# Where the raw blocks of branch a land, when the stored sums are made, and which halvings stand between drains

## The chip, the core and the metric

The kernel runs on one core of one Trainium2 chip. A core has five engines with a queue of instructions each: PE (matrix products and transposes), DVE (vector operations), ACT (activations and copies), POOL (here masks, and the issue of DMAs) and SP (here only the issue of DMAs). Each queue is worked off in order: an instruction that waits holds up everything behind it on its engine. Moved bytes go through 16 DMA engines that all queues share. The metric is the time of the whole kernel on the device in microseconds (us), the median of several runs; less is better.

## What is computed

One layer of a hybrid block over 1024 tokens of width 1024, in float32 arithmetic: a norm, a wide projection, a gated mixer of a short convolution (branch a) and a forgetting attention (branch b), an output projection, and a feed-forward net.

```python
def mixer(h, w_in, b_f, conv_w, w_branch, w_out):
    proj = jnp.einsum("bsd,dn->bsn", h, w_in)
    q, k, v, f_logit, g_b, g_c, hc, gate_conv, gate_attn = jnp.split(proj, _SPLITS, axis=-1)
    ya = g_b * causal_depthwise_conv(g_c * hc, conv_w)
    logf = jax.nn.log_sigmoid(f_logit.astype(jnp.float32) + b_f.astype(jnp.float32))
    yb = forgetting_attention(q.reshape(shp), k.reshape(shp), v.reshape(shp), logf)
    ya_d = jnp.einsum("bsc,cd->bsd", ya, w_branch[0])
    yb_d = jnp.einsum("bsc,cd->bsd", yb, w_branch[1])
    merged = jax.nn.sigmoid(gate_conv) * ya_d + jax.nn.sigmoid(gate_attn) * yb_d
    return jnp.einsum("bsd,de->bse", merged, w_out)

for l in range(DEPTH):
    m = mixer(rmsnorm(x, norm_mix_pre[l]), ...)
    x = x + rmsnorm(m, norm_mix_post[l])
    x = x + rmsnorm(swiglu(rmsnorm(x, norm_ffn_pre[l]), w_gate_up[l], w_down[l]), norm_ffn_post[l])
```

The logits of query i and key j get the bias c[i] - c[j], where c is the running sum of logf. The kernel keeps those rows of c, one per head, spread over all partitions: the forget rows, tiles `cb`.

## The kernel before, in words

**Numbers in two halves.** A float32 operand is kept as a high half (rounded by a copy, mostly on ACT) and a low half (the difference, on DVE); a product is three matmuls, high by high, high by low, low by high (`mm3`). Making both halves is called halving here (`split`, `halve`); what comes from memory is first a raw block and then halved. All engine calls go through one helper, so nearly every row of the profile has the line L76; the names of the tiles (out<-in) say which step it is.

**The stages in time.** Norm and small projections take the first 61 us. Then come 18 jobs up to about 418 us, the large projections by Strassen's scheme: seven products of 512-wide blocks in place of eight. A job has 84 matmuls of 128x512 and takes about 19 us. Its weights arrive as raw blocks (`raw<-in_w_in`, 512 KB each, on SP's queue into a few raw tiles), and DVE and ACT make their sums and halves one job ahead. The last job (`last_pair`) has the first two attention steps in it. From 416 to 566 us runs the attention loop, steps t = 2 to 22: for head pair j and some of its query rows the logits (`sp`), the row maxima on DVE (`row_max`, records CUSTOM_DVE or ISA), the exponentials on ACT (`expo`), the transposes (`tps`, drained into `ptT` by ACT and DVE) and the weighted sum with v (`po`). Each step also has one chunk of branch a (`pba`): the product of w_branch[0] with ya, again by Strassen's scheme, its seven products P1 to P7 for four pieces of the columns. After 566 us come the rest of branch a, branch b, the output projection and the feed-forward net.

**Side work in the jobs.** The sums of blocks that Strassen's scheme needs of w_branch (`wa_steps`), w_out (`wo_steps`) and ya (`ya_steps`) are made during the jobs and stored to memory (`wa_dram`, `wt_dram`, `ya_ops`) for later. Each is a generator in a few pieces. The table `plans` says which piece runs in which job: an entry (job, n) puts the next piece behind the job's addition of c12 (n = 0) or of c21 (n = 1). The raw rows of w_out go into two tiles, r0 and l0, and each piece of them ends with a store that reads them; the next `wo_steps` loads the same two tiles and so waits for those stores. In the jobs a scheduler sets the order of each queue; in the attention loop the program's order is kept on every engine.

**Around the start of attention.** Branch a's first two products need the quarter B11 of ya (P1) and B21 (P2). `load_y` fetches a quarter as a raw block (two DMAs `raw<-ya_dram`) into one of the raw tiles, and `split_y` halves it into `yB` (ACT copies, DVE subtracts). The raw tiles at that time also hold the first two attention steps' probabilities and their transposes, so a load waits for PE to be done with them. `cb_of(j, e)` loads a forget row of the head pair j into one of two `cb` tiles; `load_kv(1)` loads both forget rows, k and v of pair 1.

Of the kernel before, what the change touches and what calls it, by code (L numbers as in the profile page):

```python
# [10 lines left out]
F32 = mybir.dt.float32  # L11
# [6 lines left out]
P = 128  # L18
S = 1024
# [27 lines left out]
def block_kernel(  # L47
# [156 lines left out]
    def h_pair(name, shape):  # L204
        return [h_pool.tile(shape, F32R, name=f"{name}{t}") for t in "hl"]

# [341 lines left out]
    def flat(t):  # L548
        return t.rearrange("p a b -> p (a b)")
# [7 lines left out]
    def raw_t():  # L557
        return wtile("raw", 3)
# [156 lines left out]
    def wo_steps(k):  # L715

        both = []
        for tag, row in (("r0", k), ("l0", k + 4)):
            t = w0_tile(tag, F32)
            nc.sync.dma_start(flat(t), wout_d[row * P : (row + 1) * P, :])  # L720
            both.append(flat(t).rearrange("p (a b) -> p a b", a=2))
# [27 lines left out]
    def half_tile(t):  # L749
        return flat(t).rearrange("p (a b) -> p a b", a=2)  # L750
# [20 lines left out]
    def wa_steps(k):  # L771
# [16 lines left out]
        yield  # L788
        spill(wa_dram, 2, k, u, half_tile(w0_tile("l0")))
        yield  # L790
# [386 lines left out]
    for first, make in (  # L1177
        (((2, 0), (2, 1), (3, 0)), lambda: wa_steps(0)),
        (((3, 1), (4, 0), (4, 1)), lambda: wa_steps(1)),
        (((4, 1), (5, 0), (5, 1), (7, 0)), lambda: wo_steps(0)),  # L1180
        (((7, 1), (8, 0), (8, 1), (10, 0)), lambda: wo_steps(1)),
        (((10, 1), (11, 0), (11, 1), (12, 0)), lambda: wo_steps(2)),
        (((12, 1), (13, 0), (13, 1), (14, 0)), lambda: wo_steps(3)),
        (((10, 1), (11, 1), (12, 0), (12, 1)), lambda: ya_steps(0)),
        (((13, 1), (14, 0), (14, 1), (15, 0)), lambda: ya_steps(1)),
    ):
        it = make()
        for j, n in first:
            plans[j][n].append(it)
# [134 lines left out]
    HOME = dict(B11="h0", B21="h1", T2="l0", T3="l1", T4="h0", T1="h1", B22="l1")  # L1324
    wring, raws = deque(), {}

    def load_y(o, queue=nc.sync):
# [3 lines left out]
        if o in SUMS_Y:  # L1331
            queue.dma_start(f32(t), ya_ops[SUMS_Y.index(o)])
            return
        raws[o] = half_tile(raw_t())
        m, ns = dict(B11=(0, n1), B21=(2, n1), B22=(2, n2))[o]
# [162 lines left out]
    for t, what, p in (  # L1498
# [64 lines left out]
    cuts[2].append(do(split_y, "B21"))  # L1563
    cuts[21].append(do(split_y, "B22"))
    for t, list_ in list(chunks.items()):
        for c in list_:
            o = SEQ[c[0]][0]
            if t > 2 and o not in SUMS_W:
                cuts[t - 1].append(do(split_w, o, c[1]))
    for k, t in enumerate((16, 17, 21, 22)):  # L1570
# [10 lines left out]
    for t in (6, 8, 10, 13, 14, 20, 21, 22):  # L1581
        at[t].append(next_sg)
    at[17].append(late_sgs)
    at[15] += [do(cb_of, 3, 0, True), do(cb_of, 3, 1, True)]
    for k, t in enumerate((13, 13, 16, 16)):
# [9 lines left out]
    next_w()  # L1595
    load_kv(1)
    q_load(1)
    load_y("B21")
    lows = [split_y("B11"), split_w("A11", 0)]
    for low in lows:  # L1600
        low()
    for _ in range(3):
        next_w()
    for _ in range(4):
        next_sg()
    mask_of(2, 0)
    for t in range(2, NU + 2):
# [6 lines left out]
        if t == NU:  # L1614
            for m in [a_chunk(*c) for c in chunks.pop(t)]:
                m()
        if 5 < t <= NU:
# [7 lines left out]
        if t <= 5:  # L1625
            po_copy = pv_pair(t - 2)
        for i, e in now[0]:
            row_max(t, i, e)
        if t < NU and len(steps[t][1]) > 1 and not joined(steps[t][1]):
            mask_of(t, steps[t][1][1])  # L1630
# [888 lines left out]
```

## Time and profile before

| | |
|---|---|
| median of 3 runs | 1334.93 us (1333.1 to 1335.35) |
| the profiled execution | 1335.76 us, of which 1334.0 us lie between its first and last instruction (the span) |
| mean granted PE clock | 0.993 |
| busy share of PE, DVE, ACT, POOL | 98%, 71%, 42%, 15% |
| moved by DMA | 235.64 MB, 177 GB/s in the mean |

All times in this text are from the profiled execution, counted from its first instruction. In a timeline row the columns are start, length, engine, line, operation with out<-in and shapes, how many, and in brackets the idle time just before it with what ended it. SPq and POOLq stand for DMA issues on those queues. "x38" in a table of windows is the number of instructions that began in the window, and PEclk the clock that PE was granted, as a share of the full one.

### The profile page before, as it was taken

Reading aid. Unit: us, or ns where it says so; the run is one execution under the profiler, and the core shown is the slowest. Engines: PE = TensorE matmul, PEld = TensorE weight load, DVE = VectorE, ACT = ScalarE, POOL = GpSimd, SP = SyncE. Lnnn points to the kernel's source line nnn. Section 1 sums busy time; section 2 is a strip of 40 time slices with the busy share of each in tenths; the row PEclk is TensorE's granted clock in tenths of the full one; section 3 lists DMA queues with packets and bytes.
Section 4 is the critical chain, followed back from the end, with each engine's and each line's share of the span. In section 5 each row is a group of like instructions: output and inputs, shape, how many; then the busy total and the mean of one; then the engine's idle time right before and its main releaser. Section 6 shows DMA issues by size and latency. Waiting matters only on the chain.

```text
span 1334.0 us, 17816 instructions
## 1 busy us (share of the span) xinstructions
PE 1307.5 (98%) x6671; PEld 1086.3 (81%) x6671; DVE 948.4 (71%) x1357; ACT 565.1 (42%) x880; POOL 203.0 (15%) x371
## 2 busy tenths in 40 slices
PE   9999999998997999999999999999999999999998
PEld 8988878887886788788888878888888888888886
DVE  7876788785754577887767788867666756677574
ACT  7533232343443677522678433223222323444451
POOL 3111110122212222100223121211011101000001
PEclk9999999999999899999999999999999999999999
DMA  6356544466725564585467556533233327966541
GB/s 230 96 157 205 167 146 155 158 215 238 255 112 181 206 210 161 186 305 205 129 190 234 189 173 203 186 125 102 80 118 103 116 90 257 363 234 194 159 166 63
DMA packets 179638, 235.64 MB, mean 177 GB/s; under 512 B 12232, under 2 KB 121872, under 8 KB 179040
## 3 DMA queue, kind: packets, MB, share of 16 engines
q1 hardware_dynamic: 154544, 150.31, 35.9%
q0 software_dynamic: 24992, 84.20, 17.1%
q8 instruction: 52, 0.85, 0.3%
q14 instruction: 34, 0.28, 0.1%
q10 hardware_dynamic: 16, 0.00, 0.0%
HBM read 164.94 MB, written 69.53 MB: 176 GB/s over the span
## 4 chain that ended last, share of the span: by engine, by line
PE 92%; DVE 4%; DMA 2%; issue 1%; SPq 1%; ACT 0%; DVEq 0%; POOLq 0%; POOL 0%; ACTq 0%
PE b L76 57%; PE pd L76 16%; PE pv L76 3%; PE pbb L76 3%; PE pba L76 3%; PE tps L76 2%; PE po L76 2%; PE sp L76 2%; PE tp L76 1%; DMA raw<-in_w_in_dram 1%; PE ma L76 1%; DVE lo L76 1%; PE mb L76 1%; DMA raw<-ya_dram 1%; SPq L76 1%
## 5 line engine op out<-in xcount | busy, mean ns | idle before, releaser
L76 DVE TENSOR_TENSOR c<-c,b 128x512 f32<-128x512 f32 x215 | 146.8, 683 | 74.0 <-PE b L76 72.8
L76 DVE TENSOR_TENSOR lo<-raw,hi 128x1024 fp32r<-128x1024 f32 (+1 forms) x91 | 109.6, 1205 | 70.1 <-PE b L76 54.3
L76 ACT ACTIVATE hi<-raw 128x1024 fp32r<-128x1024 f32 (+1 forms) x98 | 99.6, 1017 | 100.4 <-PE b L76 53.8
L76 ACT ACTIVATE hi<-sx 128x1024 fp32r<-128x1024 f32 x44 | 46.7, 1062 | 192.8 <-PE b L76 166.7
L76 DVE TENSOR_TENSOR sx<-raw 128x512 f32<-128x512 f32 x78 | 53.7, 688 | 42.8 <-DMA raw<-in_w_in_dram 29.0
L76 DVE TENSOR_TENSOR lo<-sx,hi 128x1024 fp32r<-128x1024 f32 x44 | 53.8, 1223 | 38.6 <-PE b L76 37.4
L76 PE MATMUL b<-w12h,lo 128*128 128x512 f32 x208 | 80.9, 389 | 0.0
L76 PE MATMUL b<-w12h,hi 128*128 128x512 f32 x204 | 79.4, 389 | 0.0
L76 PE MATMUL b<-w12l,hi 128*128 128x512 f32 x204 | 79.4, 389 | 0.0
L76 PE MATMUL b<-hh,hi 128*128 128x512 f32 x176 | 69.0, 392 | 0.7 <-DVE c L76 0.7
L76 PE MATMUL b<-hh,lo 128*128 128x512 f32 x176 | 68.5, 389 | 0.0
L76 PE MATMUL b<-hl,hi 128*128 128x512 f32 x176 | 68.5, 389 | 0.0
L76 PE MATMUL b<-w,s4h 128*128 128x512 f32 x208 | 64.0, 389 | 0.0
L76 PE MATMUL pd<-hi,lo 128*128 128x512 f32 x160 | 62.3, 389 | 0.0
L76 PE MATMUL pd<-hi 128*128 128x512 f32 x160 | 61.9, 390 | 0.0
L76 POOL DMA_DIRECT2D a_dramA<-um x33 | 17.9, 541 | 277.2 <-DVE um L76 276.6
L76 PE MATMUL pd<-ghi 128*128 128x512 f32 x148 | 57.6, 390 | 0.0
L76 PE MATMUL pd<-ghi,glo 128*128 128x512 f32 x148 | 57.6, 389 | 0.0
L76 PE MATMUL pd<-glo,ghi 128*128 128x512 f32 x148 | 57.6, 389 | 0.0
L76 PE MATMUL b<-hT12h,lo 128*128 128x512 f32 x136 | 53.9, 396 | 3.8 <-DVE lo L76 3.7
L76 PE MATMUL b<-hT34h,hi 128*128 128x512 f32 x136 | 53.0, 390 | 0.9 <-DVE c L76 0.9
L76 PE MATMUL b<-hT12h,hi 128*128 128x512 f32 x136 | 53.4, 393 | 0.0
(487 smaller groups left out, 3601.6 us busy)
## 6 DMA issues: line engine op xcount, KB each, us to landing
raw<-in_w_gate_up_dram SPq DMA_DIRECT2D x52, 512.0 KB, 4.1
raw<-in_w_in_dram SPq DMA_DIRECT2D x35, 512.0 KB, 4.8
a_dramS<-um POOLq DMA_DIRECT2D x44, 256.0 KB, 2.9
a_dramA<-um POOLq DMA_DIRECT2D x33, 256.0 KB, 2.6
sg<-sg_dram SPq DMA_DIRECT2D x32, 256.0 KB, 5.6
graw<-a_dramS SPq DMA_DIRECT2D x14, 512.0 KB, 3.7
sg_dram<-c POOLq DMA_DIRECT2D x24, 256.0 KB, 2.5
raw<-in_w_down_dram SPq DMA_DIRECT2D x11, 512.0 KB, 6.1
```

The source lines that it names most:

```text
L76: ins = getattr(self.engine, name)(*args, **kw)
```

## The change

It has six parts, and every operation of before is still there, as often as before.

1. The tiles of `h_pair` get tags of their own, and the pool of the attention tiles sets aside its five `wraw`, two `v` and two `cb` tiles at the start.
2. The eight loads of w_out in the jobs are issued on POOL's queue in place of SP's, and `plans` is written anew: the pieces of one sum are spread over more half-jobs, and fewer sums share a half-job. One piece of the second `wa_steps` uses the tile h0 in place of l0.
3. `load_y` puts B11 and B21 into `cb` tiles (named `yraw`) and only B22 into a raw tile. The two forget rows of pair 1 are loaded in step 3, behind the last read of the raw blocks, and the other loads at the start of attention change places.
4. The low halves of B11 and of its weight, two operations on DVE, stand behind the first row maxima of step 2 in place of ahead of them.
5. In step 17 the copy `rT` stands ahead of the row maxima.
6. At step 21 P6 stands ahead of P5's last piece, B22 is halved between their two drains, and the weight halving of that step is done one step earlier.

```diff
     def h_pair(name, shape):
-        return [h_pool.tile(shape, F32R, name=f"{name}{t}") for t in "hl"]
+        return [h_pool.tile(shape, F32R, tag=f"{name}{t}", name=f"{name}{t}") for t in "hl"]
...
             t = w0_tile(tag, F32)
-            nc.sync.dma_start(flat(t), wout_d[row * P : (row + 1) * P, :])
+            nc.gpsimd.dma_start(flat(t), wout_d[row * P : (row + 1) * P, :])
...
-        spill(wa_dram, 2, k, u, half_tile(w0_tile("l0")))
+        spill(wa_dram, 2, k, u, half_tile(w0_tile(("l0", "h0")[k])))
...
         (((2, 0), (2, 1), (3, 0)), lambda: wa_steps(0)),
-        (((3, 1), (4, 0), (4, 1)), lambda: wa_steps(1)),
-        (((4, 1), (5, 0), (5, 1), (7, 0)), lambda: wo_steps(0)),
-        (((7, 1), (8, 0), (8, 1), (10, 0)), lambda: wo_steps(1)),
-        (((10, 1), (11, 0), (11, 1), (12, 0)), lambda: wo_steps(2)),
-        (((12, 1), (13, 0), (13, 1), (14, 0)), lambda: wo_steps(3)),
-        (((10, 1), (11, 1), (12, 0), (12, 1)), lambda: ya_steps(0)),
-        (((13, 1), (14, 0), (14, 1), (15, 0)), lambda: ya_steps(1)),
+        (((3, 1), (3, 1), (5, 0)), lambda: wa_steps(1)),
+        (((4, 0), (4, 1), (5, 1), (6, 1)), lambda: wo_steps(0)),
+        (((7, 0), (7, 1), (8, 0), (8, 1)), lambda: wo_steps(1)),
+        (((10, 0), (10, 1), (11, 0), (11, 1)), lambda: wo_steps(2)),
+        (((11, 0), (12, 0), (12, 1), (13, 0)), lambda: ya_steps(0)),
+        (((14, 0), (14, 0), (14, 1), (15, 1)), lambda: ya_steps(1)),
+        (((13, 1), (15, 0), (16, 0), (16, 1)), lambda: wo_steps(3)),
...
+    for tag, shape, n in (("wraw", [P, 2, P], 5), ("v", [P, ST, P], 2), ("cb", [P, S], 2)):
+        for _ in range(n):
+            t1.tile(shape, F32, tag=tag, name=tag, bufs=n)
...
-        raws[o] = half_tile(raw_t())
+        raws[o] = half_tile(
+            raw_t() if o == "B22" else t1.tile([P, ST, P], F32, tag="cb", name="yraw", bufs=2)
+        )
...
-        (18, "P4", 3), (19, "P5", 1), (20, "P5", 2), (21, "P5", 3), (21, "P6", 0),
+        (18, "P4", 3), (19, "P5", 1), (20, "P5", 2), (21, "P6", 0), (21, "P5", 3),
...
-    cuts[21].append(do(split_y, "B22"))
...
-                cuts[t - 1].append(do(split_w, o, c[1]))
+                cuts[t - 1 - (t == 21)].append(do(split_w, o, c[1]))
...
+    at[3] += [do(cb_of, 1, 0), do(cb_of, 1, 1)]
...
     next_w()
-    load_kv(1)
-    q_load(1)
     load_y("B21")
-    lows = [split_y("B11"), split_w("A11", 0)]
-    for low in lows:
-        low()
+    first_lows = [split_y("B11"), split_w("A11", 0)]
+    k_load(1)
     for _ in range(3):
         next_w()
-    for _ in range(4):
+    next_sg()
+    load_v(1)
+    q_load(1)
+    for _ in range(3):
         next_sg()
...
-            for m in [a_chunk(*c) for c in chunks.pop(t)]:
-                m()
+            p6, p5 = [a_chunk(*c) for c in chunks.pop(t)]
+            p6()
+            split_y("B22")()
+            p5()
...
+        if turned and t == 17:
+            turned()
+            turned = None
         for i, e in now[0]:
             row_max(t, i, e)
+        if t == 2:
+            for low in first_lows:
+                low()
```

The table, the placing of tiles and the written order move instructions at three places on which much rests.

**SP's queue in jobs 8 to 16, before.** `raw` are the weights of the jobs, `r` and `l` the rows of w_out for the tiles r0 and l0, `rows` two forget rows.

```order
L76 DMA l_2118<-in_w_out_dram 128x1024
L76 DMA raw<-in_w_in_dram 128x8x128 x4
L76 DMA r_2537<-in_w_out_dram 128x1024
L76 DMA raw<-in_w_in_dram 128x8x128 x2
L76 DMA l_2539<-in_w_out_dram 128x1024
L76 DMA raw<-in_w_in_dram 128x8x128 x4
L76 DMA r_2831<-in_w_out_dram 128x1024
L76 DMA l_2833<-in_w_out_dram 128x1024
L76 DMA raw<-in_w_in_dram 128x8x128 x4
L76 DMA rows_970<-c_dram 128x1024 x2
```

SP now holds 24 loads of `raw` in a row there, and the loads of w_out stand on POOL's queue, of which this is the part around jobs 10 to 13:

```order
L76 DMA wt_dram_132<-r_2472 128x1024
L76 DMA sg_dram_136<-so 128x512
L76 DMA wt_dram_133<-h_2688 128x1024
L76 DMA r_2969<-in_w_out_dram 128x1024
L76 DMA sg_dram_136<-c_2635 128x512
L76 DMA sg_dram_136<-c_2614 128x512
L76 DMA sg_dram_136<-c_2598 128x512
L76 DMA wt_dram_133<-l_2474 128x1024
L76 DMA rows_970<-ya_dram_71 128x1024
L76 DMA ya_ops<-yh 128x2x512
L76 DMA rows_970<-ya_dram_73 128x1024
```

A load of r0 or l0 now stands behind the stores of the side work and ahead of stores of the jobs' results (`sg_dram<-c`).

**SP's queue at the start of attention, before.** `qk_dram` holds q and k, `ya_dram_70` and `71` the block B11, `72` and `73` the block B21.

```order
L76 DMA v_3459<-v_dram 128x8x128
L76 DMA raw<-ya_dram_70 128x512
L76 DMA raw<-ya_dram_71 128x512
L76 DMA wraw<-in_w_branch_dram 128x2x128
L76 DMA cb<-c_dram 128x1024 x2
L76 DMA lo<-qk_dram_67 128x1024
L76 DMA v<-v_dram 128x8x128
L76 DMA raw<-qk_dram_67 128x1024
L76 DMA raw<-ya_dram_72 128x512
L76 DMA raw<-ya_dram_73 128x512
L76 DMA wraw<-in_w_branch_dram 128x2x128 x3
```

The same place now:

```order
L76 DMA v_3459<-v_dram 128x8x128
L76 DMA yraw<-ya_dram_70 128x512
L76 DMA yraw<-ya_dram_71 128x512
L76 DMA wraw<-in_w_branch_dram 128x2x128
L76 DMA yraw<-ya_dram_72 128x512
L76 DMA yraw<-ya_dram_73 128x512
L76 DMA lo<-qk_dram_67 128x1024
L76 DMA wraw<-in_w_branch_dram 128x2x128 x3
L76 DMA sg<-sg_dram_135 128x512
L76 DMA v<-v_dram 128x8x128
L76 DMA raw<-qk_dram_67 128x1024
```

The second block of ya went from behind q and v to right behind the first, and the two loads of `cb` stand further down, behind four `sg` and two `wraw`.

**DVE's queue at step 21, before.** `um` are the drains of branch a's chunks, `s4l` a weight halving, `yB` the low half of B22.

```order
L76 TENSOR_TENSOR um<-um,pba 128x512
L76 TENSOR_TENSOR um<-sg,um 128x512
L76 COPY ptT<-tps 128x512
L76 TENSOR_TENSOR s4l<-wraw,s4l 128x256
L76 TENSOR_TENSOR um<-um,pba 128x512 x2
L76 TENSOR_TENSOR um<-sg,um 128x512
L76 COPY ptT<-tps 128x128
L76 RECIPROCAL ri<-rsum 128x8
L76 COPY ptT<-tps 128x512
L76 TENSOR_TENSOR yB_5254<-raw,yB_5254 128x1024
```

The same place now:

```order
L76 TENSOR_TENSOR um<-um,pba 128x512
L76 TENSOR_TENSOR um<-sg,um 128x512
L76 COPY ptT<-tps 128x512
L76 TENSOR_TENSOR um<-um,pba 128x512
L76 TENSOR_TENSOR um<-sg,um 128x512
L76 TENSOR_TENSOR yB_5265<-raw,yB_5265 128x1024
L76 TENSOR_TENSOR um<-um,pba 128x512
L76 COPY ptT<-tps 128x128
```

The weight halving left this stretch for the step before, and the low half of B22 moved up between the two drains, ahead of the transposes' copies.

## The prediction

> **What bounds the kernel now.** I read the page's shares first, then the waits of PE.
>
> ```profile
> span 1334.0 us, 17816 instructions
> PE 1307.5 (98%) x6671; PEld 1086.3 (81%) x6671; DVE 948.4 (71%) x1357; ACT 565.1 (42%) x880; POOL 203.0 (15%) x371
> ...
> PE tps L76 <- ACT ptT L76: 4.9, 1, 4.9
> PE pba L76 <- ACT s L76: 4.6, 1, 4.6
> PE b L76 <- DVE lo L76: 3.7, 1, 3.7
> PE b L76 <- DVE c L76: 1.7, 2, 0.9
> ...
> PE pba L76 <- ACT yB L76: 0.9, 1, 0.9
> PE pba L76 <- DVE s4l L76: 0.9, 1, 0.9
> PE pba L76 <- DVE yB L76: 0.8, 1, 0.8
> PE pba L76 <- DVE rT L76: 0.7, 1, 0.7
> ```
>
> PE is busy for 98% of the span, and the change takes no matmul away, so only two things can shorten the time: PE's few idle stretches, and slow matmuls after them. A row of the second view gives us in total, times, longest. Three single waits are long: one in the jobs (b, for a low half) and two at the start of attention (pba and tps). The rest are below 1 us each. So I followed those three back, each on the queue of its releaser.
>
> **The wait in the jobs.** These are rows of the timelines of POOL, SP, DVE and PE, then two of the chain of waits, one of the DMA issues (its last number is the median us to landing), and one of the table of windows (length, busy us of PE, PEld, DVE, ACT, POOL, granted clock, share of the DMA engines, GB/s).
>
> ```profile
> 298.93 0.57 POOL L76 DMA_DIRECT2D wt_dram<-l  x1 [1.20 <-DVE l L76]
> ...
> 306.33 0.34 SPq L76 DMA_DIRECT2D l<-in_w_out_dram  x1
> 306.78 13.40 SPq L76 DMA_DIRECT2D raw<-in_w_in_dram  x2
> ...
> 302.08 1.23 DVE L76 TENSOR_TENSOR lo<-raw,hi 128x1024 fp32r<-128x1024 f32 x1 [1.83 <-PE b L76]
> ...
> 315.71 0.39 PE L76 MATMUL b<-hT12l,hi 128*128 128x512 f32 x1
> 319.83 0.80 PE L76 MATMUL b<-hT12h,lo 128*128 128x512 f32 x1 [3.73 <-DVE lo L76]
> ...
> 322.98 0.40 PE L76 MATMUL b<-hT12h,hi 128*128 128x512 f32 x1
> ...
> 299.78 5.00 PE b L76 x22
> ...
> 306.78 9.60 DMA raw<-in_w_in_dram
> ...
> raw<-in_w_in_dram SPq DMA_DIRECT2D x35, 512.0 KB, 4.8
> ...
> 300.00:310.00 10.00, 10.00 (x46) 8.29 (x45) 3.99 (x5) 3.87 (x5) 4.18 (x7) 1.00 0.98 333
> ```
>
> Read from the end. PE waits 3.73 us for a low half, the last of a row of DVE operations that began when its raw block had landed (306.78 + 9.60 = 316.38). That raw block could have been fetched when DVE had read its tile (302.08 + 1.23 = 303.3), but SP's queue stood at the load of l0, which waits until the store of the old l0, issued at 298.93, is done. So the block was issued 306.78 - 303.3 = 3.5 us late, among transfers that kept the DMA engines 98% busy. The cost is more than the wait: 22 matmuls usually take 5.00 us, 0.227 each, but from 315.71 to 322.98 only eight begin, 7.27 - 8 x 0.227 = 5.45 us lost. The first seven after the wait ran slow.
>
> By the Trainium skill ("TensorE: Matmul & The Clock Gate", section "What's actually happening") PE falls to half clock after about 3.4 us without work and needs about as long under load to come back, so each such stall would cost up to 1.7 us beyond itself. The trace agrees here: 5.45 - 3.89 (the gap from 315.71 to 319.83 less one matmul) = 1.56.
>
> **The start of attention.**
>
> ```profile
> 398.97 0.37 SPq L76 DMA_DIRECT2D v<-v_dram  x1
> ...
> 418.99 0.81 SPq L76 DMA_DIRECT2D raw<-ya_dram  x2
> ...
> 422.42 3.86 SPq L76 DMA_DIRECT2D raw<-qk_dram  x1
> 426.45 0.79 SPq L76 DMA_DIRECT2D raw<-ya_dram  x2
> ...
> 426.82 7.45 DMA raw<-ya_dram
> ...
> 400.00:410.00 10.00, 10.00 (x50) 7.69 (x48) 5.02 (x8) 2.39 (x4) 1.98 (x4) 1.00 0.25 84
> ...
> 416.35 0.33 PE L76 MATMUL sp<-hi 64*128 64x128 f32 x2
> ...
> 425.38 2.93 PE L76 MATMUL pba<-yB,s 128*128 128x512 f32 x6 [4.58 <-ACT s L76]
> ...
> 436.25 0.90 PE L76 MATMUL tps<-ident,rows 128*128 128x128 f32 x3 [4.86 <-ACT ptT L76]
> ...
> 443.60 0.50 PE L76 MATMUL sp<-hi 64*128 64x512 f32 x2
> ...
> 462.88 0.33 PE L76 MATMUL sp<-hi 64*128 64x128 f32 x2
> ...
> 475.68 0.50 PE L76 MATMUL sp<-hi 64*128 64x512 f32 x2
> ```
>
> SP issues nothing between 399 and 419, since B11 goes into a raw tile that PE still reads, while the DMA engines are a quarter busy. Then ten loads go out at once. B11 is issued at 418.99, and PE's first branch chunk waits 4.58 us for it. B21 is issued at 426.45, behind a q load that held the queue for 3.86 us, and takes 7.45 us to land; ACT, in order, halves it ahead of the copy `ptT`, for which PE waits 4.86 us. Steps 2 and 3 are rows (5, 0) and (4, 1) of pair 0; steps 7 and 8 are the same rows of pair 1, with chunks of the same six matmuls. From the first logits of step 2 to those of step 4 it is 443.60 - 416.35 = 27.25 us, from step 7 to step 9 it is 475.68 - 462.88 = 12.80. So 14.45 us are lost: 4.58 + 4.86 = 9.44 of idling and 5.0 of slow matmuls (six in 2.93 us).
>
> By the same rule of the skill the two stalls would lose at most 9.44 + 2 x 1.7 = 12.8 us. The rows say 14.45, and I take the rows; by the rule the forecast below would be 1.6 us later.
>
> **What each part does to the time.** *Loads of w_out on POOL, new plans.* SP's queue holds only weights there, so the raw block goes out at 303.3; even with the same 9.60 us it lands at 312.9, and the 3.5 us saved nearly cover the 3.73 us lost. The new table has the second ya sum and the last w_out sum elsewhere, so the fetch has fewer neighbours. Bounds: nothing, if the DMA engines are as full in another way, and 5.45. I take 5.4, because a block 0.2 us late leaves no clock to lose. Of the two waits for `c`, the 0.9 us one in job 6 comes from a copy of l0 that waited for its load; l0 is now fetched two pieces ahead. Bounds 0 and 0.9, I take 0.7. The other 0.8 us in that row lies behind the attention and stays. The price of eight more issues on POOL is read from the nearest row:
>
> ```profile
> L76 POOL DMA_DIRECT2D sg_dram<-c x24 | 13.1, 545 | 67.7 <-ACT c L76 64.5 <-DVE c L76 3.2
> ```
>
> 8 x 0.545 = 4.4 us on an engine that is 15% busy: nothing, as long as no load stands waiting at the head of that queue (a rival below).
>
> *Raw blocks in `cb` tiles.* These tiles lie where the jobs' operands were, so B11 can be issued behind v at 399.4, weights and B21 behind it, while the DMA engines are a quarter busy; both land before 415. The probabilities' tiles are no longer waited for. What is late next at step 2 is DVE, which has to do the first maxima and then the two low halves (below also the forget rows' first users, on POOL and DVE):
>
> ```profile
> 424.49 1.23 DVE L76 TENSOR_TENSOR yB<-raw,yB 128x1024 fp32r<-128x1024 f32 x1 [7.34 <-ACT yB L76]
> ...
> 425.97 0.95 DVE L76 CUSTOM_DVE_ANT_0 rows<-sp,rows 128x768 f32<-128x768 f32 x1
> ...
> 447.51 0.88 POOL L76 TENSOR_TENSOR cb<-cb,mask 128x128 f32<-128x128 f32 x2
> ...
> 451.75 1.22 DVE L76 CUSTOM_DVE_ANT_0 pt<-sp,cb 128x1024 f32<-128x1024 f32 x1 [0.79 <-issue]
> ```
>
> The logits end near 418.0; one maximum in its two pieces 1.1, the low halves 1.23 and a third of that: 420.7, where PE comes from `po` at about 420.8. So at most 0.1 there. Putting these halves ahead (as before) would have cost nothing either, so part 4 only lets the maxima, and with them the next transposes, start 1.6 us earlier. I take 14.0 of the 14.45: 0.45 for DVE, whose two maxima and three halvings of full length alone take 2 x 1.1 + 3 x 1.2 = 5.8 us of a 6.4 us step, with several small operations beside them. Bounds: half of it (7), if a later load takes the wait's place, and 14.45. (Times here are those of before; where I say so, with the 14 us taken out.) The two forget rows of pair 1 now go out as late as about 421 and 426.5, when DVE has read the raw blocks; with 7.45 us they land by 434. Their first user masked them at 447.51, which with the 14 us out is 433.5, and was done 3.4 us before the maximum that reads them. So a landing by 437 costs nothing, and that is 3 us of cover.
>
> *Step 17.* `rT` ahead of two maxima removes the 0.7 us wait, but the second maximum then ends as before and holds the next logits' bank. Bounds 0 and 0.7, I take 0.4.
>
> *Step 21.* The waits for `s4l` and for `yB` on ACT and on DVE are 0.9 + 0.9 + 0.8 = 2.6 us.
>
> ```profile
> 544.14 1.10 POOL L76 DMA_DIRECT2D raw<-ya_dram  x2 [0.51 <-ACT ptT L76]
> ...
> 556.42 1.05 ACT L76 ACTIVATE yB<-raw 128x1024 fp32r<-128x1024 f32 x1
> ```
>
> B22 was issued at 544.14 but halved at 556.42 only, behind a copy that waited for PE. Halved between the drains it is done by about 554.5, before P7 at some 556, unless it takes over 9 us to land. The halving moved to the step before lies where PE waits for nothing. I take 2.5 (bounds 0 and 2.6). Part 1 moves addresses only: nothing.
>
> **The sum.** 5.4 + 0.7 + 14.0 + 0.4 + 2.5 = 23.0 us. From the profiled execution 1335.76 - 23.0 = 1312.8; that execution stands 0.83 above the median of the runs, so the forecast is 1312 us. Behind 566 us PE is full, with all its loads issued relative to the same work, so an earlier start should carry through whole. The forecast's own range takes 4.5 to 5.45, 0 to 0.9, 12 to 14.45, 0 to 0.7 and 1 to 2.6, not all at one end, and 1 us for the spread of the runs: 1310 to 1316.
>
> **Rivals.** *The job's block stays late (1317).* For it: the engines were 98% busy at 300 to 310, and 9.60 us is twice the median 4.8. Against: the side work beside it is spread over more jobs. Then 5.4 are missing.
>
> For this rival speaks a rule of the Trainium skill ("DMA: Bandwidth & Descriptors", section "Issuing engines are not separate DMA queues"): another issuing engine saves only the time of issuing, since all transfers share the same 16 DMA engines. By it the move to POOL would be worth one 0.34 us issue; but the row at 306.33 shows a queue held for 3.5 us by a wait, of which that section says nothing.
>
> *A new wait at steps 2 to 5 (1319).* The forget rows, q or DVE's own order take the place of the raw blocks, and half of the 14 us comes back. The point from which it decides is a forget row that lands after 437. For it: slack of 3 us only, and DVE's load; against: from 399 to 419 SP's queue was idle and the DMA engines three quarters free, and part of the loads now goes there.
>
> *POOL's queue blocks (slower, 1339).* A load of r0 or l0 at its head waits for a store's landing, and the stores of results behind it free their tiles too late for the next job, so that DVE's additions and then PE stop. Each such stop costs what the one above did, 5.45 us; from five of the eight loads on it outweighs the 23.0 (5 x 5.45 = 27, 1312 + 27 = 1339). For it: POOL's order, with loads between result stores. Against: a tile is needed again only a job later, 84 x 0.227 = 19 us, while the SP wait for such a store was 3.5 us.
>
> *Nothing gained (1335).* The raw blocks' new tiles would still be held by the last job until 419. The order of products speaks against it.
>
> **How the numbers follow.** Forecast 0.66, late block 0.10, new wait 0.15, POOL 0.06, nothing 0.03. The median of the runs varies by about 2 us, so 0.2% (2.7 us) is what can be told from no change. Faster by more than that is the sum of the first three, 0.91; within it 0.03; slower 0.06. The range holds the forecast's own, the late block and most of the new wait's: 1308 to 1322, with 0.02 left below and some 0.15 above.
>
> **What would show it.** Right: the timeline of SP with `yraw` loads near 400; step 2's logits to step 4's 12.8 to 14 us; no PE wait above 1 us from 300 to 450; a granted clock of 1.00 in every window of the jobs and of 420 to 450; P7 begun about 22 us earlier than in the profile of before. Wrong: a wait of PE in the jobs released by `c` or `lo` with POOL's queue standing at `in_w_out`, or DVE waiting for `cb` at step 4 or 5.

## The result, and the profile after

The changed kernel takes 1313.4 us in the median (1313.07 to 1313.45, 4 runs) against 1335.14 us before (1333.1 to 1337.99): a ratio of 0.9835 with a 95% interval of 0.9817 to 0.9853, 21.7 us less. The forecast was 1312 us, with a range of 1308 to 1322. The profiled execution took 1313.38 us, with a span of 1311.6 us against 1334.0.

First the page of the changed kernel and then its waits of PE (us in total, times, longest). Of the two waits over 4 us and the one of 3.7 us nothing is left but 0.9 us in the jobs, and two short waits for `um` are new.

```profile
span 1311.6 us, 17809 instructions
...
PE 1300.4 (99%) x6671; PEld 1081.7 (82%) x6671; DVE 947.8 (72%) x1357; ACT 564.6 (43%) x880; POOL 207.1 (16%) x379
```

```profile
...
PE pba L76 <- DVE um L76: 1.0, 2, 0.6
PE b L76 <- DVE lo L76: 0.9, 1, 0.9
PE b L76 <- DVE c L76: 0.7, 1, 0.7
```

Where the time went is read from PE's timeline at marks that both kernels have. After:

```profile
315.93 0.50 PE L76 MATMUL b<-hT12h,lo 128*128 128x512 f32 x1 [0.88 <-DVE lo L76]
...
410.67 0.33 PE L76 MATMUL sp<-hi 64*128 64x128 f32 x2
...
423.81 0.50 PE L76 MATMUL sp<-hi 64*128 64x512 f32 x2
...
527.46 1.63 PE L76 MATMUL pba<-yT,s4l 128*128 128x512 f32 x6
...
536.60 0.27 PE L76 MATMUL tr<-ident,ri 128*8 128x128 f32 x1
538.70 1.65 PE L76 MATMUL pba<-yT,s4h 128*128 128x512 f32 x6 [0.58 <-DVE um L76]
...
543.75 1.42 PE L76 MATMUL pba<-yB,s 128*128 128x512 f32 x5 [0.46 <-DVE um L76]
```

And the two marks of the kernel before that were not shown yet, the branch chunk of step 20 and the transpose behind P7:

```profile
547.10 1.63 PE L76 MATMUL pba<-yT,s4l 128*128 128x512 f32 x6
...
560.05 0.27 PE L76 MATMUL tr<-ident,ri 128*8 128x128 f32 x1
```

| mark | before | after | lead | won since the mark above | forecast |
|---|---|---|---|---|---|
| logits of step 2 (end of the jobs) | 416.35 | 410.67 | 5.7 | 5.7 | 6.1 |
| logits of step 4 | 443.60 | 423.81 | 19.8 | 14.1 | 14.0 |
| branch chunk of step 20 | 547.10 | 527.46 | 19.6 | -0.2 | 0.4 |
| transpose behind P7 | 560.05 | 536.60 | 23.5 | 3.8 | 2.5, with the next row |
| end of the span | 1334.0 | 1311.6 | 22.4 | -1.1 | |
| sum | | | | 22.4 | 23.0 |

SP's timeline at the start of attention shows the raw blocks 25 and 31 us earlier than before, in a stretch where the DMA engines had been a quarter busy before (0.25 from 400 to 410); the forget rows follow at 416:

```profile
393.76 0.99 SPq L76 DMA_DIRECT2D yraw<-ya_dram  x2
...
395.41 1.08 SPq L76 DMA_DIRECT2D yraw<-ya_dram  x2
...
416.38 4.36 SPq L76 DMA_DIRECT2D cb<-c_dram  x2
```

Of the 5.7 us of the jobs, 1.0 was won ahead of the late block (its tile is free at 302.08 + 1.23 before and 301.04 + 1.23 after; forecast 0.7) and 4.6 at it (forecast 5.4).

The terms came out near their forecasts in this comparison of two profiles, and every sign that the prediction named for being right is there: `yraw` loads near 394, 13.14 us from the logits of step 2 to those of step 4, no wait above 0.9 us and a granted clock of 1.00 from 300 to 450, P7 begun 22.4 us earlier (535.13 against 557.52). Whether the terms came out so for the reasons given is another question, and for the jobs the answer is no: all these signs would be there whether the queue or the table had freed the late block.

### The profile page after: what moved, and what is told of

The parts are those of the page before. It is cut to its first block, busy times and chain, and to the rows that moved or that the text cites. A ratio compares the mean times of both kernels' runs of the same rounds, so it can differ in the third digit from the quotient of the medians.

```text
span 1311.6 us, 17809 instructions
## 1 busy us (share of the span) xinstructions
PE 1300.4 (99%) x6671; PEld 1081.7 (82%) x6671; DVE 947.8 (72%) x1357; ACT 564.6 (43%) x880; POOL 207.1 (16%) x379
## 4 chain that ended last, share of the span: by engine, by line
PE 96%; DVE 2%; DMA 1%; issue 0%; ACT 0%; SPq 0%; DVEq 0%; POOLq 0%; POOL 0%; ACTq 0%
PE b L76 61%; PE pd L76 16%; PE pv L76 3%; PE pbb L76 3%; PE pba L76 3%; PE po L76 3%; PE tps L76 3%; PE sp L76 2%; PE tp L76 1%; PE ma L76 1%; PE mb L76 1%; DMA raw<-in_w_gate_up_dram 0%; DVE um L76 0%; DMA wr<-in_w_in_dram 0%; DVE lo L76 0%
## 5 line engine op out<-in xcount | busy, mean ns | idle before, releaser
L76 PE MATMUL b<-hT12l,hi 128*128 128x512 f32 x136 | 52.9, 389 | 0.0
```

Of the source, the lines that this page charges most:

```text
L76: ins = getattr(self.engine, name)(*args, **kw)
```

## The experiments

Each run was timed between runs of the kernel before on the same chip. Medians of the kernel before were 1334.88, 1335.71 and 1335.57 us in the three groups, with single runs from 1331.7 to 1339.8.

### What freed the late block in the jobs: the queue or the table?

Part 2 moves the loads of w_out to POOL's queue and rewrites the table. Four runs take it apart. All of part 2 and nothing else:

```diff
-            nc.sync.dma_start(flat(t), wout_d[row * P : (row + 1) * P, :])
+            nc.gpsimd.dma_start(flat(t), wout_d[row * P : (row + 1) * P, :])
...
+        ... the new table of `plans`, and h0 for l0 in the second wa_steps
```

> The kernel before with part 2 alone (loads of w_out on POOL, the new table, tile h0). My theory: the waits are separate and their costs add up, so this part is worth what the logits of step 2 gained between the two profiles, 416.35 - 410.67 = 5.7 us: 1329.4 us, with one wait of about 0.9 us left in the jobs near 315 us and the two long waits at the start of attention as before (4.6 and 4.9 us). Rival: the gain of the jobs came from the transfers being fewer beside the late block thanks to the tiles of part 1; then this part alone leaves the 3.7 us wait and gives 1335 us.

Measured: 1329.22 us, ratio 0.9950 (0.9933 to 0.9968), and no stall near 315 us. Step 2 begins at 410.57 us, against 410.67 in the changed kernel. So part 2 alone makes the whole gain of the jobs, as expected.

The queue alone, with the old table:

```diff
-            nc.sync.dma_start(flat(t), wout_d[row * P : (row + 1) * P, :])
+            nc.gpsimd.dma_start(flat(t), wout_d[row * P : (row + 1) * P, :])
```

> The kernel before with the eight loads of w_out on POOL's queue and the old table. My theory (a queue held by a waiting load): the raw block of job 14 goes out about 3.5 us earlier, near 303 us, and most of the 5.45 us stall goes: 1330 to 1331 us, the small wait for c in job 6 may stay. Rival (the 16 DMA engines are shared, the queue is only the time of issuing): no change, 1335 us, the block still lands after 316 us.

Measured: 1335.95 us, ratio 1.0006 (0.9995 to 1.0018). No change, as the rival said. Rows of this run's DVE, SP, POOL and PE timelines, with the block's transfer from the chain of waits:

```profile
303.43 1.23 DVE L76 TENSOR_TENSOR lo<-raw,hi 128x1024 fp32r<-128x1024 f32 x1 [1.83 <-PE b L76]
...
316.77 0.69 DVE L76 TENSOR_TENSOR sx<-raw 128x512 f32<-128x512 f32 x1 [8.72 <-DMA raw<-in_w_in_dram]
...
318.11 0.68 DVE L76 TENSOR_TENSOR c<-c,b 128x512 f32<-128x512 f32 x1
...
319.42 0.69 DVE L76 TENSOR_TENSOR s<-raw,sx 128x512 f32<-128x512 f32 x1
320.03 1.22 DVE L76 TENSOR_TENSOR lo<-raw,hi 128x1024 fp32r<-128x1024 f32 x1
...
304.72 0.37 SPq L76 DMA_DIRECT2D raw<-in_w_in_dram  x1
...
304.24 0.54 POOL L76 DMA_DIRECT2D l<-in_w_out_dram  x1 [1.50 <-DMA wt_dram<-l]
304.77 1.05 POOL L76 DMA_DIRECT2D rows<-ya_dram  x2
...
304.72 11.93 DMA raw<-in_w_in_dram
...
321.30 0.50 PE L76 MATMUL b<-hT12h,lo 128*128 128x512 f32 x1 [3.85 <-DVE lo L76]
```

The same DVE operations before:

```profile
316.49 0.69 DVE L76 TENSOR_TENSOR sx<-raw 128x512 f32<-128x512 f32 x1 [8.28 <-DMA raw<-in_w_in_dram]
...
318.55 1.22 DVE L76 TENSOR_TENSOR lo<-raw,hi 128x1024 fp32r<-128x1024 f32 x1
319.69 0.68 DVE L76 TENSOR_TENSOR c<-c,b 128x512 f32<-128x512 f32 x1
```

The block goes out at 304.72, 0.06 us after its tile is free (303.43 + 1.23), so nothing holds SP any more. But it takes 11.93 us in place of 9.60, which uses up 2.3 of the 3.5 us saved. Of the rest, 1.1 us arrive at DVE: it first uses the block (`sx`) 12.1 us after the tile is free, against 13.2 before. They are lost there. The scheduler put two operations, `c` and `s`, ahead of the low half that stood behind it before, so the low half is done 4.5 us after the first use in place of 3.3, and PE waits 3.85 us all the same. So freeing the queue did what was said of it and bought nothing: the block waited among the transfers, and its low half in DVE's queue. On what the move is worth, the Trainium skill was right against the prediction ("DMA: Bandwidth & Descriptors", section "Issuing engines are not separate DMA queues"): the transfers of all queues interleave on the same 16 engines.

The table alone, with the loads on SP:

```diff
-        (((12, 1), (13, 0), (13, 1), (14, 0)), lambda: wo_steps(3)),
-        (((13, 1), (14, 0), (14, 1), (15, 0)), lambda: ya_steps(1)),
+        (((14, 0), (14, 0), (14, 1), (15, 1)), lambda: ya_steps(1)),
+        (((13, 1), (15, 0), (16, 0), (16, 1)), lambda: wo_steps(3)),
...
```

> The kernel before with the new table and tile h0, loads of w_out still on SP's queue. My theory: a load of l0 that waits for a store still holds up the weights behind it on SP, so a stall of PE stays or moves to another job: between 1331 and 1336 us. Rival (the table, by fewer transfers at one time, makes the whole gain): 1329.5 us, as with both.

Measured: 1326.7 us, ratio 0.9936 (0.9920 to 0.9952). The rival, not my theory, and 2.5 us below part 2 alone. In the profiles 1.3 us lie in the jobs and 1.5 us in steps 2 and 3 (25.3 against 26.7 us), which neither run changes. Of this run:

```profile
298.53 0.34 SPq L76 DMA_DIRECT2D l<-in_w_out_dram  x1
302.19 0.37 SPq L76 DMA_DIRECT2D raw<-in_w_in_dram  x1
...
300.90 1.23 DVE L76 TENSOR_TENSOR lo<-raw,hi 128x1024 fp32r<-128x1024 f32 x1 [2.03 <-PE b L76]
...
309.95 0.69 DVE L76 TENSOR_TENSOR sx<-raw 128x512 f32<-128x512 f32 x1 [4.44 <-DMA raw<-in_w_in_dram]
```

The load of l0 stands on SP here, ahead of the block, and does not hold it: it went out at 298.53, and the block at 302.19, as soon as its tile was free. Step 2 begins at 409.35 us, 1.3 us earlier than in the changed kernel. The last run of this group leaves the loads on POOL and changes one row of the table:

```diff
-        (((12, 1), (13, 0), (13, 1), (14, 0)), lambda: wo_steps(3)),
+        (((13, 1), (15, 0), (16, 0), (16, 1)), lambda: wo_steps(3)),
```

> The kernel before with the loads of w_out on POOL and one row of the table changed: the last w_out sum starts a job later, so that its two loads of 512 KB leave the stretch in which the late block of job 14 is fetched. Against the run with POOL's queue and the old table (1335.95 us, a wait of 3.9 us, the block 11.9 us under way) nothing else differs there. Theory now (the block shares the DMA engines with what is in flight): 1 MB less at about 340 GB/s is 3 us, so the block takes about 9 us, the wait falls to 1 us or less and no slow clock follows: 1331 to 1332.5 us. Rival (the DVE operations ahead of the low half, or the rest of the table, make the wait): the 3.9 us stay, 1336 us.

Measured: 1333.24 us, ratio 0.9986 (0.9973 to 0.9999), so 2.7 us less than with the queue alone by the medians, but not by the stated way. The wait near 319 us is still 3.23 us, and the block took 11.3 us. The load of r0 moved only from 302.18 to 308.54, still beside the block. The "1 MB less" was a miscount, and this run does not decide on its own.

All runs together do, for the table as a whole. The next table counts, for each kernel, the transfers of 512 KB for the side work (w_out, ya and their stores) that were issued between 9 us before the block's tile was free and its landing, and the time from the tile being free (the end of `lo<-raw`) to DVE's first use of the block (`sx<-raw`):

| kernel | w_out loads | table | held on SP, us | side transfers | tile free to first use, us | PE waits, us |
|---|---|---|---|---|---|---|
| before | SP | old | 3.5 | 10 | 13.2 | 3.7 |
| parts 1 and 3 (below) | SP | old | 3.4 | 10 | 13.8 | 4.3 |
| queue only | POOL | old | 0.1 | 10 | 12.1 | 3.9 |
| one row | POOL | old, one row new | 0.1 | 9 | 11.5 | 3.2 |
| the change | POOL | new | 0.1 | 6 | 9.1 | 0.9 |
| part 2 alone | POOL | new | 0.1 | 6 | 7.4 | none |
| table only | SP | new | 0.1 | 6 | 7.8 | none |

By these rows the hold on SP is worth 1 to 2 us of landing, and four transfers fewer are worth 3 to 5. That it is the number of transfers, and not something else in the new table, is the reading that fits; the one run that was to vary it alone changed it only from 10 to 9. In all of them but the first two the low half is done 4.5 us after the first use, and a block in use within about 8 us costs nothing.

In the changed kernel the load of l0 goes out 1 us behind the block and shares the engines with it; on SP it went out 4 us ahead. (In part 2 alone it goes out 1 us behind as well, and there the block is in use after 7.4 us.) That led to this run, the changed kernel with the loads back on SP:

```diff
-            nc.gpsimd.dma_start(flat(t), wout_d[row * P : (row + 1) * P, :])
+            nc.sync.dma_start(flat(t), wout_d[row * P : (row + 1) * P, :])
```

> The changed kernel with the eight loads of w_out back on SP's queue, the new table kept. Theory now (transfers beside the late block, not the queue): the load of l0 goes out some 4 us before the block rather than 1 us behind it, the 0.9 us wait near 315 us goes, and the jobs gain 7.0 in place of 5.7 us, as with the table alone: 1312.1 us. Rival (the theory of the prediction, a queue held by a waiting load): a load of r0 or l0 waits for its store at the head of SP's queue and holds up weights, a stall of 1 to 5 us comes back: 1314.5 to 1319 us.

Measured: 1311.65 us (1310.94 to 1314.32), ratio 0.9826 (0.9808 to 0.9844). Its profile has no wait in the jobs at all, the block is in use 7.9 us after its tile is free, and step 2 begins at 409.24 us, 1.4 us ahead of the changed kernel. The intervals of the two ratios overlap, so the times alone do not show it faster; but there is no sign of the 1 to 5 us that the queue theory asks for.

Nor do the profiles show that SP is the better queue. The jobs of the changed kernel also stand, unchanged, in the five runs below that alter only what comes behind them, and with the loads on SP once more in the last run. Counted from the first matmul of the jobs to the logits of step 2:

| kernels | w_out loads | table | jobs, us | tile free to first use, us | wait at the late block, us |
|---|---|---|---|---|---|
| before; parts 1 and 3 | SP | old | 355.7, 358.0 | 13.2, 13.8 | 3.7, 4.3 |
| queue only; one row | POOL | old, or one row new | 357.2, 355.0 | 12.1, 11.5 | 3.9, 3.2 |
| the change, part 2 alone and five more | POOL | new | 349.1 to 350.3 | 7.4 to 9.6 | none to 1.4 |
| table only and two more | SP | new | 348.7 to 349.1 | 7.8 to 8.4 | none to 0.2 |

The table is worth 5 us or more on either queue. With the new table the two queues differ by less than the profiles with POOL do among themselves, so the 0.9 us in the changed kernel's profile cannot be laid to the queue.

### What the start of attention is worth by itself

Parts 1 and 3 alone:

```diff
-        raws[o] = half_tile(raw_t())
+        raws[o] = half_tile(
+            raw_t() if o == "B22" else t1.tile([P, ST, P], F32, tag="cb", name="yraw", bufs=2)
+        )
...
+    ... tiles set aside, cb of pair 1 in step 3, loads in the new order
```

> The kernel before with parts 1 and 3 alone (tiles set aside, raw blocks in cb tiles, new order of the loads); the low halves stay ahead of the first maxima. My theory: both long waits go and the clock with them, 14.1 us: 1321.0 us. Rival A (the maxima behind the low halves become the next wait): 1 to 1.6 us less gained, 1322 to 1322.7 us. Rival B (only the idling goes, the slow matmuls there are due to something else, as the busy DMA engines): 9.4 us, 1325.7 us.

Measured: 1323.25 us, ratio 0.9914 (0.9897 to 0.9930): 11.6 us, between my theory and rival B. The profile tells them apart, with the marks of this run:

```profile
321.73 0.50 PE L76 MATMUL b<-hT12h,lo 128*128 128x512 f32 x1 [4.29 <-DVE lo L76]
...
418.48 0.33 PE L76 MATMUL sp<-hi 64*128 64x128 f32 x2
...
432.09 0.50 PE L76 MATMUL sp<-hi 64*128 64x512 f32 x2
```

Steps 2 and 3 take 432.09 - 418.48 = 13.6 us against 27.25 before: 13.6 us won, with the slow matmuls gone as well as the idling. The 2 us that the time lacks are not found so surely. In this profile the jobs are slower than before, with step 2 at 418.48 against 416.35, 4.29 us at the late block, and a second wait for a low half (6.2 us in two). But this execution took 1325.66 us, 2.4 more than the median, and the slow matmuls that it also has at step 21 (below) are part of that; what the jobs cost in the other executions is not on record. Both stretches vary by 1 to 2 us between kernels that are the same there. Steps 2 and 3, where unchanged, take 27.25 us before and 26.7, 25.6, 25.4 and 25.3 us in the four runs of part 2 and of pieces of it: by those the two steps are worth 12 to 14 us, and the profile of before stood at the long end.

The last 0.5 us from 13.6 to 13.1 is part 4. The changed kernel with the low halves ahead of the maxima again:

```diff
-    first_lows = [split_y("B11"), split_w("A11", 0)]
+    lows = [split_y("B11"), split_w("A11", 0)]
+    for low in lows:
+        low()
...
-        if t == 2:
-            for low in first_lows:
-                low()
```

> The changed kernel with part 4 undone: the low halves of B11 and its weight ahead of the first maxima on DVE. By the prediction this order is worth nothing (1313.4 us). By the profile of the run with parts 1 and 3 alone, whose steps 2 and 3 took 13.6 us against 13.1 in the changed kernel, it is worth 0.5 us: 1313.9 us, with a wait of PE for ptT of 0.2 to 0.3 us near 419 us. Rival: the maxima, 1.6 us later, hold the next logits as well: 1315 us.

Measured: 1312.97 us (1311.38 to 1313.76), ratio 0.9829 (0.9813 to 0.9846). The profile has the 0.5 us (424.53 - 410.89 = 13.64 us for steps 2 and 3) and this one wait:

```profile
420.00 0.55 PE L76 MATMUL tps<-ident,rows 128*128 128x128 f32 x3 [0.23 <-ACT ptT L76]
```

The time does not show it. Part 4 is worth nothing that can be measured in the time.

### Step 17 and step 21

Part 5 undone (`rT` behind the row maxima of step 17 again):

```diff
-        if turned and t == 17:
-            turned()
-            turned = None
```

> The changed kernel with part 5 undone (rT behind the row maxima in step 17). The prediction gave it 0.4 us (1313.8 us). By the two profiles the lead won at rT, 0.6 us, is given back at the logits of the next step, which begin 0.6 us later than they could: 1313.4 us, no difference.

Measured: 1313.25 us, ratio 0.9833 (0.9816 to 0.9849), no difference. The same stretch of PE without and, in the second fence, with the change:

```profile
508.70 0.28 PE L76 MATMUL tr<-ident,ri 128*16 128x128 f32 x1
...
509.97 1.66 PE L76 MATMUL pba<-yT,s 128*128 128x512 f32 x6 [0.67 <-DVE rT L76]
...
513.31 0.88 PE L76 MATMUL po<-ptT,v 128*64 128x128 f32 x12
```

```profile
508.97 0.28 PE L76 MATMUL tr<-ident,ri 128*16 128x128 f32 x1
...
509.62 1.65 PE L76 MATMUL pba<-yT,s 128*128 128x512 f32 x6
...
511.53 0.90 PE L76 MATMUL sp<-hi 64*128 64x448 f32 x2
...
513.38 0.88 PE L76 MATMUL po<-ptT,v 128*64 128x128 f32 x12
```

From `tr` to `po` it is 4.61 us without and 4.41 us with part 5. The 0.67 us wait is gone, and the next logits begin early but run long (0.90 us against the 0.47 of the same row before): on DVE the second maximum, whose bank they need, began at 510.63 and took 1.21 us.

Part 6 undone:

```diff
-            p6, p5 = [a_chunk(*c) for c in chunks.pop(t)]
-            p6()
-            split_y("B22")()
-            p5()
+            for m in [a_chunk(*c) for c in chunks.pop(t)]:
+                m()
...
+    cuts[21].append(do(split_y, "B22"))
```

> The changed kernel with part 6 undone (P5's last piece ahead of P6, B22 halved with the step's other halvings). Theory: the three waits of 0.9, 0.9 and 0.8 us come back, and the two waits for um of 0.6 and 0.5 us go, so 2.4 to 2.8 us: 1315.8 to 1316.2 us. Rival: one of the three waits came from the work being late by the earlier stalls; then less than 1.5 us.

Measured: 1317.82 us (1315.53 to 1319.36), ratio 0.9867 (0.9849 to 0.9886): 4.4 us more than the changed kernel, where 2.4 to 2.8 were expected. The three waits are back; and behind them this run's matmuls are slow:

```profile
537.58 0.50 PE L76 MATMUL pba<-yB,s4h 128*128 128x512 f32 x1 [0.87 <-ACT yB L76]
538.84 1.75 PE L76 MATMUL pba<-yB,s4h 128*128 128x512 f32 x5 [0.76 <-DVE yB L76]
...
540.74 2.40 PE L76 MATMUL po<-ptT,v 128*64 128x128 f32 x20
...
540.00:550.00 10.00, 10.00 (x53) 0.84 0.79 281
```

In the last row the columns are length, busy us of PE, granted clock, DMA share and GB/s. The 20 matmuls of `po` take 2.40 us here, with a granted clock of 0.84 from 540 to 550. In the profile of before the same group took 1.31 us behind the same waits. Seven profiles have this pair of waits, 0.87 and 0.76 us with one matmul of 0.50 us between them. In five the clock stays at 1.00 in the five microseconds behind them; in this one and in that of parts 1 and 3 alone it is 0.66, with the five matmuls behind the second wait at 1.75 us and here:

```profile
547.25 2.29 PE L76 MATMUL pba<-yB,s4h 128*128 128x512 f32 x5 [0.76 <-DVE yB L76]
```

So waits below 1 us can cost clock too, in some executions and not in others.

### How long a wait has to be to cost clock

The changed kernel with the high copy of B11 made n times more on ACT, so that PE waits in step 2 for a time that we choose; the DMA engines are not full there (0.68 busy from 410 to 420 and 0.41 from 420 to 430 in the changed kernel).

```diff
+    for _ in range(3):   # 6 in the second run
+        copy(yops["B11"][:, 0], raws["B11"])
     first_lows = [split_y("B11"), split_w("A11", 0)]
```

> The changed kernel with the high copy of B11 on ACT made three times more, 3 x 0.95 us ahead of the first branch chunk of step 2. PE then waits there for about 2.3 us in all. Theory (a wait of PE costs a slow stretch behind it only when it is long): no slow matmuls, cost 2 to 2.5 us: 1315.7 us. Rival (any wait of that size is followed by slow matmuls): 4 us, 1317.4 us.

> The changed kernel with the high copy of B11 made six times more: PE waits for about 5.2 us in step 2. Theory (slow clock behind long waits, as read from the profile of before): six matmuls of the chunk take 2.5 to 3 us in place of 1.6 and the next two groups are slow as well, 1.5 to 2.5 us on top: 1320 to 1321 us. Rival (the slow matmuls in the kernel before came from the busy DMA engines, which are not busy here): 5.2 us alone, 1318.6 us.

Measured: 1317.25 us (ratio 0.9863, 0.9843 to 0.9883) with three copies, and 1320.71 us (0.9884, 0.9868 to 0.9900) with six. With three:

```profile
416.58 0.50 PE L76 MATMUL pba<-yB,s 128*128 128x512 f32 x1 [1.46 <-ACT s L76]
417.54 2.50 PE L76 MATMUL pba<-yB,s 128*128 128x512 f32 x5 [0.45 <-DVE yB L76]
...
427.60 0.50 PE L76 MATMUL sp<-hi 64*128 64x512 f32 x2
...
410.00:420.00 10.00, 8.09 (x71) 0.87 0.63 201
```

With six:

```profile
419.47 0.80 PE L76 MATMUL pba<-yB,s 128*128 128x512 f32 x1 [4.72 <-ACT s L76]
420.42 2.50 PE L76 MATMUL pba<-yB,s 128*128 128x512 f32 x5 [0.16 <-DVE yB L76]
...
420.00:430.00 10.00, 9.84 (x72) 0.76 0.33 119
```

| | PE waits, us | steps 2 and 3 longer by, us | slow running, us |
|---|---|---|---|
| three copies | 1.46 + 0.45 = 1.9 | 427.60 - 410.66 - 13.14 = 3.8 | 1.9 |
| six copies | 4.72 + 0.16 = 4.9 | 430.88 - 410.28 - 13.14 = 7.5 | 2.6 |

(13.14 is the changed kernel's 423.81 - 410.67.) Six copies speak for the clock and against the DMA engines as the cause of the slow matmuls: they run slow at a DMA share of 0.33. Three copies speak for the rival, 1317.4 us: 1.9 us of waiting cost as much again.

### A version that beats both?

The changed kernel with the loads on SP and, in step 22, one halving moved behind the drain of P7, since the waits for `um` were new:

```diff
+        if t == NU:
+            late_lows, lows = lows, []
...
-            for m in muls:
+            for m in muls + late_lows:
                 m()
```

> The changed kernel with the loads of w_out on SP's queue (1311.65 us) and, in step 22, the low half of the third row of w_branch[1] behind the drain of P7 on DVE in place of ahead of it. Theory: the first of the two waits for um (0.6 us) goes, the second stays, since DVE has as much to do: 1311.1 us. Rival (the moved halving makes the second wait longer by as much): 1311.7 us.

Measured: 1313.27 us (1311.33 to 1316.36), ratio 0.9831 (0.9809 to 0.9853). The first wait for `um` went and the second grew from 0.46 to 1.09 us: the rival. DVE is as full as in the changed kernel (34 of the 40 us from 520 to 560 in both), and here the order only picked which product waits. Neither this version nor the one with the loads on SP alone (1311.65 us) is shown to beat the change.

## Why the prediction was right, and where it was not

**The start of attention (14.0 forecast, 14.1 between the two profiles): right, for the stated reason.** The raw blocks in `cb` tiles went out at 393.8, both waits went, and the slow matmuls behind them went too; parts 1 and 3 alone gave 13.6 of it. That the comparison of equal steps (27.25 against 12.80 us) was the way to price idling and slow running together held up: 9.4 us of waits were worth 14 in that execution. That forecast and result agree to 0.1 us is no proof of the size, since both are taken from the same profile of before; by the median of the runs, parts 1 and 3 gave 11.6. Of the 0.45 us put down to DVE, 0.3 were lost (13.14 against 12.80). The forget rows, put at a landing by 434 with the 14 us out, delayed nothing.

**The jobs (6.1 forecast, 5.7 measured): the size was right and the cause wrong.** That SP's queue stood at the load of l0 and the block was issued 3.5 us late was read rightly: with the queue free it goes out 0.06 us after its tile is. The step that failed is the next one, "even with the same 9.60 us it lands at 312.9, and the 3.5 us saved nearly cover the 3.73 us lost". Freeing the queue alone saved nothing (ratio 1.0006): the block's transfer grew from 9.60 to 11.93 us, issued earlier among the same transfers, and the remaining 1.1 us went in DVE's order. What freed the block was the table, which alone gives 0.9936 and takes the side transfers around the block from 10 to 6; the prediction gave that one sentence. Its lower bound, "nothing, if the DMA engines are as full in another way", is what the queue alone came to, and the rival of the late block, put at 0.10, had the mechanism of the queue right, though not the outcome, since the table came with it. So that this term came out near its size was in good part luck. Whether POOL's queue is any better or worse than SP's with the new table, neither the times nor the ten profiles tell.

**Step 17 (0.4 forecast): nothing that the time shows (0.2 us between the profiles).** I had named what holds it, the second maximum, and should have taken the lower bound.

**Step 21 (2.5 forecast, 3.8 - 1.1 = 2.7 in the profile): right as a sum.** The three waits went. What came in their place, two waits for `um` of 0.58 and 0.46 us, I had not named. Undoing it cost 4.4 us by the medians: the profile of that run also has slow matmuls behind the waits, a cost that the prediction's bound of 2.6 left out without a reason.

**The carry through the rest: right but for the 1.1 us just named.** Behind the waits for `um` both kernels take the same 763.6 us to the end.

**The total (23.0 forecast, 21.7 measured): partly luck.** By the medians of the runs the parts are worth 5.7 (part 2 alone), 11.6 (parts 1 and 3 alone), nothing (parts 4 and 5) and 4.4 (part 6), which add up to the 21.7. Against the forecast's 6.1, 14.0, 0.4 and 2.5 the start was put too high and step 21 too low by some 2 us each, and the two offset each other. Each of these prices is uncertain by about 2 us itself (an interval of 0.0016 to 0.0019 on each ratio), so this is an indication and not shown.

**The other rivals.** A new wait at steps 2 to 5 did not come, for a forget row or anything else. POOL's queue did block once, in the run with the queue alone and at a small price: there a load of l0 stood behind a store that waited for DVE, went out at 162.52 us against 160.44 on SP before, and PE's wait for `c` in job 6 was 1.58 us in place of 0.94. In the change, whose table starts the loads earlier, this wait is gone.

## What to carry to other kernels

A transfer that is late because its queue was held need not be early when the queue is freed: look first at how much else is in flight in the ten microseconds around it, and move that. A wait of the matmul engine is priced by comparing the same steps with and without it, not by its idle time, since slow running behind it can cost as much again; and by more than one profile, since the same stretch varied here by 2 us. Where DVE is nearly full, moving an operation out of the way of one wait can make the next one longer.

## What was not expected of the hardware

With the copies, waits of 1.46 + 0.45 us were followed by 1.9 us of slow running and waits of 4.72 + 0.16 us by 2.6 us; the granted clock was 0.87 and 0.76 in those ten microseconds. Waits of 0.87 and 0.76 us, close together, were followed by a full clock in five profiles and by a fall in two. Single waits of up to 1.96 us (parts 1 and 3 alone, at 125 us) left it at 1.00. Whether the clock falls is thus not settled by the length of a wait; what one fall takes was much the same each time. Summed over the windows of ten microseconds, the granted clock lacks 1.7 us at each of three falls: before at the late block (0.98 and 0.85 from 310 to 330), with three copies (0.87 and 0.96 from 410 to 430) and with part 6 undone (0.99 and 0.84 from 530 to 550).

The Trainium skill ("TensorE: Matmul & The Clock Gate", section "What's actually happening") has the clock fall after about 3.4 us without work, in a window that runs freely. The freely running window fits the profiles that differ behind the same waits, though no run here shows the window itself; the figure of 3.4 us of idling is too long for these runs.

The four runs of the changed kernel lie between 1313.07 and 1313.45 us, those of the kernel before between 1331.7 and 1339.8. That the long waits make this spread is not shown: the two kernels with the loads on SP have none of them either, and their four runs each spread over 3.4 and 5.0 us.
